# Fetching expert tokens by indirect DMA, and 512-column token-major projections, in a two-layer encoder trunk

## The chip, the cores and the metric

One core of one Trainium2 chip. The metric is device time in microseconds of one launch. The kernel before takes 1617.72 us (median of 3 runs, 1615.04 to 1621.96). The execution that was profiled took 1623.95 us.

## The reference

Two layers work on 512 tokens of 1024 features in float32. Each layer mixes tokens (gated linear attention, mLSTM and latent attention side by side, all reading the same input), projects the result back, adds a residual and normalises; then cross-attends to 256 memory tokens; then runs a mixture of experts: each token picks one of 4 groups and the two best of that group's 8 experts.

```
y = x @ w_in                                   # columns shared out among three mixers
x = LN(ALPHA * x + concat(mixers(y)) @ w_out)
x = LN(ALPHA * x + cross_attention(x, mem) @ w_o)
for e in range(32):                            # gate is 0 for all but two experts of a token
    h = silu(t @ w_gate[e]) * (t @ w_up[e])
    out = out + (h @ w_down[e]) * gate[:, e:e + 1]
x = LN(ALPHA * x + out)
```

## The kernel before, in words

Tokens are four tiles of 128. Everything but the experts is projected in three matmuls per product (`mm3`, L383): weights and activations are split into a rounded part and a rest, and hi x hi, lo x hi and hi x lo are summed in PSUM. Weights come in pieces of 128 x 1024 values (512 KB), loaded on SP's queue (L359) into `raw`, split by ScalarE (L350, `whi`) and VectorE (L351, `wlo`).

*Token-major projections.* The values and gates of two mixers (L850 to L854, L932 to L935), the output projection and the cross-attention's output projection (both in `proj_residual`, L469) give results with tokens on partitions. They are cut into groups of 256 columns: `tm_weights` (L414) splits the two pieces of a group, `tm_tile` (L417) runs 8 x 3 matmuls of 256 columns for each token tile. There are 2 + 2 + 4 + 4 groups a layer, so 12 x 4 x 24 = 1152 matmuls.

*Experts.* Every expert has 64 slots. The router (`router_tile`, L1147) gives each token's two choices a slot number. A pair of experts, 128 slots, is one iteration of the loop in `moe` (L1421), 16 a layer. A pair's weights are twelve pages of 512 KB: eight of gate and up (`in_gu`), four of down (`in_dn`). They are loaded on SP's queue (L1351) into a ring of 22 pages (`moe_raw`, L369): free pages of five tags and one tile of four pages, `raw4`, tag `T16`. A page is loaded again as soon as the matmuls that read it are done; SP issues in ring order.

TensorE's order in an iteration is the program's: the down-projection of the pair before (L1383), the up-projection of this pair (L1360), and then a last phase in which the pair before is added into the tokens (`scatter`, L1502, 16 matmuls of 512 columns, each bank then added by VectorE at L1506) and four chunks of the next four experts' tokens are gathered (`gather`, L1320). The gather is a matmul with a one-hot matrix: for each of 8 feature chunks, 2 (hi, lo) x 4 (token tiles) matmuls of 256 columns, whose one-hot VectorE builds (`slots_onehot`, L1279, `onehot_tile`, L1205). So it makes 64 matmuls for every two pairs, for slots 256 to 2047. The first 256 slots are gathered by `gather_first` (L1289) inside the router's last tiles.

*The end of a layer.* In layer 0 the last iteration starts a piece of the next layer's memory projection (`fill_ahead`, L1391), whose matmuls (tile `fb`) fill TensorE between the last scatters. Slots beyond 64 of an expert are computed after the loop in `overflow` (L1538), a loop with a count from the data: here none in layer 0, one in layer 1. GpSimd builds its one-hots (`overflow_block`, L1522 and L1523), TensorE gathers (`gather_few`, L1331) and runs one expert on 64 slots (L1558, L1571, L1580). Then comes `last_norm` (L1593).

Of the kernel before, what the change touches and what calls it, by code (L numbers as in the profile page):

```python
# [38 lines left out]
FAR = 16384  # L39
MLA_SCALE = float(96 ** -0.5)  # L40
# [69 lines left out]
def pack(x, mem, positions, w_in, w_out, gla_w_a2, gla_b_a, gla_norm_g, ml_conv_w, ml_b_i, ml_b_f, ml_norm_g,  # L110
# [23 lines left out]
    def tm(l, i, w):  # L134
        for g in range(w.shape[1] // 256):
            a = w[:, g * 256:(g + 1) * 256].reshape(2, 4, P, 256).transpose(0, 2, 1, 3).reshape(2, P, 1024)
            pieces[l, i + 2 * g:i + 2 * g + 2] = a
# [3 lines left out]
    for l in range(L):  # L141
# [18 lines left out]
        tm(l, PI_XV, arr["xkv"][l][:, D:])  # L160
# [48 lines left out]
class K:  # L209
# [50 lines left out]
    def setup(self):  # L260
        nc, a = self.nc, self.a
        self.const = self.cp.tile([P, NCO], F32, name="const")
        self.ident = self.c("ident")
        self.vec = [self.cp.tile([P, N_VC], F32, name=f"vec{l}") for l in range(L)]
        for l in range(L):
            nc.sync.dma_start(self.vec[l], a["cols"][l])
        nc.sync.dma_start(self.const, a["consts"])
        self.ones16 = self.cp.tile([P, P], F16, name="ones16")
        nc.vector.tensor_copy(self.ones16, self.c("ones"))
        self.zero16 = self.cp.tile([P, P], F16, name="zero16")  # L270
        nc.vector.memset(self.zero16, 0.0)
# [3 lines left out]
        nc.vector.tensor_copy(self.e64, self.c("e64", 1))  # L275
        self.mhalf = self.cp.tile([P, 1], F32, name="mhalf")
        nc.vector.memset(self.mhalf, -0.5)
# [91 lines left out]
    def moe_raw(self):  # L369
# [4 lines left out]
        i = self.n_raw % (len(ring) + 4)  # L374
# [4 lines left out]
        if i == len(ring):  # L379
            self.raw4 = self.t([P, 4, 1024], "T16", 4, pool=self.tp)  # L380
        return self.raw4[:, i - len(ring), :]
# [32 lines left out]
    def tm_weights(self, i, page=None):  # L414
        return [[v.rearrange("p (k c) -> p k c", k=4) for v in self.piece(i + j, page)] for j in range(2)]

    def tm_tile(self, w, xT, t):  # L417

        ps = self.bank(self.pj)[:, 0:256]
        for k in range(KC):  # L420
            self.mm3(ps, [v[:, k, t * P:(t + 1) * P] for v in xT], [v[:, k % 4, :] for v in w[k // 4]], k == 0, k == KC - 1)
# [47 lines left out]
    def proj_residual(self, l, piece0, srcT, x, ln, xT, page):  # L469
# [3 lines left out]
        st = [self.t([P, 4, 6], "ln_st", 4) for _ in range(NT)]  # L473
# [9 lines left out]
        def add(g, t, w):  # L483
            xs = x[t][:, g * 256:(g + 1) * 256]
            nc.vector.scalar_tensor_tensor(xs, xs, ALPHA, self.tm_tile(w, srcT, t), op0=OP.mult, op1=OP.add)
            nc.vector.bn_stats(st[t][:, g, :], xs)

        for g in range(2):
            w = self.tm_weights(i + 2 * g)
            for t in range(NT):  # L490
                add(g, t, w)
        w = [self.tm_weights(i + 4), self.tm_weights(i + 6, page)]
        for t in range(NT):
            for g in range(2):
                add(2 + g, t, w[g])
                if g == 0 and t:
                    finish(t - 1)
# [335 lines left out]
    def gla(self, l, xT):  # L833
# [15 lines left out]

        for t, ps in self.tm_group(base + PI_GVR, xT):  # L850
            nc.scalar.copy(V[:, t, :], ps)
        for t, ps in self.tm_group(base + PI_GVR + 2, xT):
            nc.scalar.activation(gate[:, t, :], ps, AF.Tanh, scale=0.5)
            nc.vector.scalar_tensor_tensor(gate[:, t, :], gate[:, t, :], 1.0, ps, op0=OP.add, op1=OP.mult)  # L854
# [57 lines left out]
    def mlstm(self, l, xT, mixT):  # L912
# [19 lines left out]
        for t, ps in self.tm_group(base + PI_MVO, xT):  # L932
            nc.scalar.copy(V[:, t, :, 0:64], ps.rearrange("p (h w) -> p h w", h=4))
        for t, ps in self.tm_group(base + PI_MVO + 2, xT):
            nc.scalar.activation(gate[:, t, :], ps, AF.Tanh, scale=0.5)  # L935
# [211 lines left out]
    def router_tile(self, x, t, st, r):  # L1147
# [8 lines left out]
        nc.scalar.activation(x, x, AF.Identity, scale=rs, bias=nm)  # L1156
        uT = self.t([P, KC, P], "e_y", 2, pool=self.mp)
# [121 lines left out]
    def slots_onehot(self, s, base, n):  # L1279
# [3 lines left out]
        nc.vector.tensor_scalar(sq, s, float(-base), None, op0=OP.add)  # L1283
        oh = self.t([P, NT, n], "oh", 2, F32R, self.mp)
        for t in range(NT):
            self.onehot_tile(oh[:, t, :], sq[:, t, :])
        return oh
# [24 lines left out]

    def gather(self, l, Xs, oh, n, X, chunks, run):

        nc, v = self.nc, self.vec[l]
        for f in chunks:
            ps = self.bank()[:, 0:n]
            for i in range(2):
                for t in range(NT):
                    run.append(nc.tensor.matmul(ps, X[i][t][:, f * P:(f + 1) * P], oh[:, t, :],  # L1320
                                                start=i + t == 0, stop=i + t == NT))
            self.gathered(l, Xs, f, ps)

    def gather_few(self, l, Xs, oh, X):

        nc, v = self.nc, self.vec[l]
        for hf in range(2):
            ps, rows = self.bank()[0:CAP, :], self.t([P, T], "e_s", 4, pool=self.mp)[0:CAP, :]
            for i in range(2):
                for t in range(NT):  # L1330
                    nc.tensor.matmul(ps, oh[:, t, :], X[i][t][:, hf * 512:(hf + 1) * 512], start=i + t == 0, stop=i + t == NT)  # L1331
            self.copy(rows, ps, "ad"[hf])
            ps = self.bank()
            for k in range(4):
                nc.tensor.transpose(ps[:, k * CAP:(k + 1) * CAP], rows[:, k * P:(k + 1) * P], self.ident[0:CAP, 0:CAP])
            for k in range(4):
                f = 4 * hf + k
                nc.scalar.activation(Xs[:, f, :], ps[:, k * CAP:(k + 1) * CAP], AF.Identity,
                                     scale=v[:, VC_LG + f:VC_LG + f + 1], bias=v[:, VC_LB + f:VC_LB + f + 1])
# [69 lines left out]
    def moe(self, l, r, X, x, following):  # L1409
# [3 lines left out]
        XX = self.t([P, 2, KC, 4 * CAP], "T16", 4, pool=self.tp)  # L1413
        ohs = [r["oh0"]]
        add = self.gather_first(l, XX[:, 0], ohs[0], X)
        for t in range(NT):
            add(t)
        ws = self.t([P, NE // 2], "rws")
        last = NE // 2 - 1
        self.marks, before = True, None  # L1420
        for p in range(NE // 2):  # L1421
            q, pr = p // 2, p % 2
            e = 2 * p
            if p == last:
                self.fill = iter(())
                if following and self.n_gap:
                    self.fill_ahead(following)
            up, act, turn, down, y = self.experts(
                XX[:, q % 2, :, 128 * pr:128 * pr + 128], [a["gu"][l * NE + e + i] for i in range(2)],
                [a["dn"][l * NE + e + i] for i in range(2)], ws[:, p:p + 1], self.moe_raw,  # L1430
                None if p < last else lambda: self.t([P, 1024], "e2", self.n_e2, pool=self.e2))
# [7 lines left out]
            act()  # L1439
            if p == 0:  # L1440
# [5 lines left out]
            full = []  # L1446
            if q < NE // 4 - 1:
                if pr == 0:
                    ohs.append(self.slots_onehot(s, 256 * (q + 1), 256))
                full = [lambda run, c=4 * pr + i, o=ohs[-1], X2=XX[:, (q + 1) % 2]: self.gather(l, X2, o, 256, X, (c,), run)  # L1450
                        for i in range(4)]
# [21 lines left out]
        self.overflow(l, r, X, x, sums)  # L1473
# [36 lines left out]
    def overflow_block(self, l, r, X):  # L1510
# [6 lines left out]
        o2 = self.t([P, 2, NT, 2, CAP], "oh", 2, pool=self.mp)  # L1517
        oh = self.t([P, NT, 2, CAP], "oh", 2, F32R, self.mp)
# [5 lines left out]
        self.gather_few(l, Xs, oh[:, :, 0, :], X)  # L1524
# [7 lines left out]
        for t in range(NT):  # L1532
            nc.tensor.transpose(ps[:, t * P:(t + 1) * P], oh[:, t].bitcast(F32).rearrange("p a b -> p (a b)"), self.ident)
        nc.scalar.copy(ohT, ps)
        nc.gpsimd.tensor_scalar(so, so, float(-CAP), None, op0=OP.add)
        return Xs, ws, ohT

    def overflow(self, l, r, X, x, sums):  # L1538
# [3 lines left out]
        with self.tc.For_i(0, n, 1) as i:  # L1542
# [10 lines left out]
            Xs, ws, ohT = self.overflow_block(l, r, X)  # L1553
# [144 lines left out]
    def run(self, layers=L):  # L1698
# [3 lines left out]
        self.kvd = self.dp.tile([4, P, 1024], F32, name="kvd")  # L1702
        self.early = {PI_MISC: self.raw_piece(PI_MISC)}
# [24 lines left out]
```

## Time and profile before

| | |
|---|---|
| time of the profiled execution | 1623.95 us |
| span, first to last instruction | 1622.1 us |
| granted TensorE clock, mean | 0.978 |
| busy: matmuls / weight loads | 1555.0 us (96%) / 1151.0 us (71%) |
| busy: VectorE / ScalarE / GpSimd | 1067.8 us / 575.9 us / 32.5 us |
| DMA | 303.04 MB, mean 187 GB/s |

Matmuls are pipelined, so a row's own duration is its latency; what one costs in a stream is the distance from one start to the next. TensorE is busy nearly all the time, which tells where to look but not what a change in one stage is worth: the mixers move 20 to 180 GB/s in a 40th of the span, the expert loops 240 to 380.

### The profile page before, as it was taken

The page shows a single profiled execution, that of the slowest core. Times are in us where ns is not written, and L with a number is a line of the kernel's source. Part 1 is how long each engine was busy: PE and PEld are TensorE (multiplying, and loading weights), DVE is VectorE, ACT ScalarE, POOL GpSimd, SP SyncE. Part 2 cuts the span into 40 slices and gives each one's busy share as a digit, 9 for nine tenths or more (in the row PEclk, how much of TensorE's full clock was granted, in tenths as well). Part 3 has the DMA queues.
Part 4 walks back from the last instruction along what each step waited for, and adds up shares of the span by engine and source line. Part 5 has one row for each costly group of instructions (what it writes and reads, how often), then busy time and mean ns, then how long its engine had stood idle before and what let it go on. Part 6 is the DMA issues. An engine that isn't in the chain of part 4 may idle for free. (4 is left out here: it accounts for less than half of the span.)

```text
span 1622.1 us, 25953 instructions
## 1 busy us (share of the span) xinstructions
PE 1555.0 (96%) x10270; PEld 1151.0 (71%) x10270; DVE 1067.8 (66%) x2352; ACT 575.9 (36%) x1026; POOL 32.5 (2%) x44
## 2 busy tenths in 40 slices
PE   7999999999999999999889999999999999999994
PEld 6988876898896555555579888669889855555542
DVE  6768678675568954445767857777655798545454
ACT  6434346324323222222463442552342332222212
POOL 0000000010000000000000000001000000000100
PEclk9999899999999999999999989999999999999997
DMA  6432220522437999996543332033224599899861
GB/s 218 149 119 80 79 72 20 177 68 82 155 121 268 381 341 343 342 352 247 212 152 106 104 98 93 6 122 94 92 86 153 184 351 373 326 339 346 333 238 53
DMA packets 90656, 303.04 MB, mean 187 GB/s; under 512 B 10404, under 2 KB 10916, under 8 KB 90404
## 3 DMA queue, kind: packets, MB, share of 16 engines
q1 hardware_dynamic: 90532, 301.36, 52.7%
q8 instruction: 81, 1.33, 0.3%
q14 instruction: 43, 0.35, 0.1%
HBM read 292.93 MB, written 8.39 MB: 186 GB/s over the span
## 5 line engine op out<-in xcount | busy, mean ns | idle before, releaser
L386 PE MATMUL pj<-whi,T 128*128 128x256 f32 x640 | 183.4, 287 | 4.5 <-ACT T L846 2.8
L1506 DVE TENSOR_TENSOR e<-e,sm 128x512 f32<-128x512 f32 x240 | 153.2, 683 | 51.1 <-PE sm L1502 50.7
L388 PE MATMUL pj<-wlo,T 128*128 128x256 f32 x640 | 182.9, 286 | 3.8 <-DVE wlo L351 3.8
L387 PE MATMUL pj<-whi,T 128*128 128x256 f32 x640 | 182.4, 285 | 0.0
L386 PE MATMUL pj<-T,whi 128*128 128x512 f32 (+1 forms) x368 | 135.3, 368 | 5.9 <-ACT T L350 5.6
L1502 PE MATMUL sm<-e_y,e_oT 128*128 128x512 f32 x512 | 139.3, 397 | 1.3 <-ACT e_y L1385 0.8
L351 DVE TENSOR_TENSOR wlo<-raw,whi 128x1024 fp32r<-128x1024 f32 x86 | 104.7, 1221 | 51.2 <-ACT whi L350 50.7
L387 PE MATMUL pj<-T,wlo 128*128 128x512 f32 (+1 forms) x368 | 135.9, 370 | 2.3 <-DVE wlo L351 2.3
L1320 PEld LDWEIGHTS sm<-oh,T 128*128 128x128 f32 x896 | 117.5, 188 | 25.7 <-issue 17.8
L388 PE MATMUL pj<-T,whi 128*128 128x512 f32 (+1 forms) x368 | 135.0, 368 | 0.0
L1320 PE MATMUL sm<-oh,T 128*128 128x256 f32 x896 | 129.6, 287 | 0.0
L386 PEld LDWEIGHTS pj<-whi,T 128*128 128x128 f32 x640 | 123.9, 194 | 5.8 <-ACT T L846 3.0
L388 PEld LDWEIGHTS pj<-wlo,T 128*128 128x128 f32 x640 | 123.8, 194 | 5.3 <-DVE wlo L351 5.1
L350 ACT CAST whi<-raw 128x1024 fp32r<-128x1024 f32 x86 | 89.8, 1048 | 105.2 <-PE pj L387 57.4
L387 PEld LDWEIGHTS pj<-whi,T 128*128 128x128 f32 x640 | 123.9, 194 | 0.2
L1360 PE MATMUL pj<-e,T 128*64 128x512 f32 x448 | 110.2, 593 | 0.0
L1310 ACT ACTIVATE T<-sm,vec 128x256 f32<-128x256 f32 x116 | 65.3, 566 | 105.1 <-PE sm L1320 105.1
L1502 PEld LDWEIGHTS sm<-e_y,e_oT 128*128 128x128 f32 x512 | 88.1, 188 | 20.4 <-ACT e_y L1385 3.3
L1368 DVE TENSOR_TENSOR e_sl<-e_sl,pj 128x256 f32<-128x256 f32 x32 | 13.5, 421 | 132.7 <-ACT e_sl L1367 132.6
L1385 ACT ACTIVATE e_y<-pj,rws 128x512 fp32r<-128x512 f32 x64 | 43.8, 687 | 118.6 <-PE pj L1383 106.7
L1360 PEld LDWEIGHTS pj<-e,T 128*64 128x64 f32 x448 | 35.1, 137 | 69.9 <-issue 67.7
L386 PEld LDWEIGHTS pj<-T,whi 128*128 128x128 f32 x368 | 70.5, 192 | 17.5 <-ACT T L350 6.4
(483 smaller groups left out, 3200.0 us busy)
## 6 DMA issues: line engine op xcount, KB each, us to landing
e<-in_gu SPq DMA_DIRECT2D x112, 512.0 KB, 9.3
raw<-in_pieces SPq DMA_DIRECT2D x94, 512.0 KB, 3.6
e<-in_dn SPq DMA_DIRECT2D x60, 512.0 KB, 7.6
T<-in_gu SPq DMA_DIRECT2D x44, 512.0 KB, 7.4
wlo<-in_gu SPq DMA_DIRECT2D x36, 512.0 KB, 8.9
whi<-in_gu SPq DMA_DIRECT2D x34, 512.0 KB, 8.8
raw<-in_gu SPq DMA_DIRECT2D x34, 512.0 KB, 8.5
fw<-in_pieces SPq DMA_DIRECT2D x60, 256.0 KB, 3.0
```

The source lines that it names most:

```text
L350: self.nc.scalar.copy(hi, src)
L351: self.nc.vector.tensor_tensor(lo, src, hi, op=OP.subtract)
L386: mm(ps, a[0], b[0], start=first, stop=False)
L387: mm(ps, a[1], b[0], start=False, stop=False)
L388: return mm(ps, a[0], b[1], start=False, stop=last)
L1310: self.nc.scalar.activation(Xs[:, f, :], ps, AF.Identity, scale=v[:, VC_LG + f:VC_LG + f + 1], bias=v[:, VC_LB + f:VC_LB + f + 1])
L1320: run.append(nc.tensor.matmul(ps, X[i][t][:, f * P:(f + 1) * P], oh[:, t, :], start=i + t == 0, stop=i + t == NT))
L1360: run.append(nc.tensor.matmul(st["h"][CAP * i:CAP * i + CAP, :], Xs[:, k, i * CAP:(i + 1) * CAP], st["w"][i][:, (k % 2) * 512:(k % 2 + 1) ...
L1368: nc.vector.tensor_tensor(sl[0:R], sl[0:R], st["h"][0:R, DE:], op=OP.mult)
L1385: nc.scalar.activation(y[0][0:R, c], po[0:R, :], AF.Copy, scale=ws)
L1502: m = nc.tensor.matmul(ps, ohT[:, t * P:(t + 1) * P], y[i][0:n, c], start=i == 0, stop=i == 1)
L1506: nc.vector.tensor_tensor(x[t][:, c], x[t][:, c], ps, op=OP.add)
```

## The change

In the experts, `router_tile` writes each normalised token tile to a table in DRAM (`ud`) from ScalarE's queue. For every two pairs VectorE builds the same one-hots as before, now in 16 bits; eight one-column matmuls turn them into token numbers (`slot_tokens`); and GpSimd clears a 128 x 1024 tile and fetches a pair's tokens into it by indirect DMA (`fetch`; an empty slot has a number out of bounds and stays zero). The fetch for pair p+3 is issued at the end of iteration p. In iteration p TensorE transposes the rows of pair p+1 in two groups of four (`fetched`), ScalarE applies the norm's gain and bias. `gather` and `gather_few` are gone, `gather_first` stays. As the split tokens are not read after the first gather, the ring of weight pages grows from 22 to 30. `fill_ahead` starts after the last pair's up-projection, and the last pair's down weights come from the ring. The overflow block takes its one-hots' space from `e_y`, the tag of the scatter's operands, and fetches its 64 tokens by indirect DMA.

The token-major projections take 512 columns a matmul. `tm_group` holds four banks and goes weight piece by weight piece over all four token tiles; in `proj_residual` the second half goes tile by tile, the last tile in two halves of 256.

```diff
     def moe_raw(self):
-        i = self.n_raw % (len(ring) + 4)
+        i = self.n_raw % (len(ring) + 12)
...
     def tm_group(self, i, xT):
-        w = self.tm_weights(i)
-        for t in range(NT):
-            yield t, self.tm_tile(w, xT, t)
+        ps = [self.bank(self.pj) for _ in range(3)] + [self.bank()]
+        for j in range(4):
+            w = self.tm_weights(i + j)
+            for t in range(NT):
+                for k in (2 * j, 2 * j + 1):
+                    self.mm3(ps[t], [v[:, k, t * P:(t + 1) * P] for v in xT], [v[:, k % 2, :] for v in w], k == 0, k == KC - 1)
+        return ps
...
         nc.scalar.activation(x, x, AF.Identity, scale=rs, bias=nm)
+        nc.scalar.dma_start(self.ud[self.l][t * P:(t + 1) * P, :], x)
...
+    def slot_tokens(self, s, q, oh):
+        nc.vector.tensor_scalar(sq, s, float(-256 * q), None, op0=OP.add)
         for t in range(NT):
             self.onehot_tile(oh[:, t, :], sq[:, t, :])
+        def tokens(run):
+            ps = self.bank()
+            for pr in range(2):
+                for t in range(NT):
+                    run.append(nc.tensor.matmul(ps[:, pr:pr + 1], oh[:, t, pr * P:(pr + 1) * P], self.tok16[:, t:t + 1],
+                                                start=t == 0, stop=t == NT - 1))
+            ix = self.t([P, 2], "gix", 3, I32)
+            nc.vector.tensor_scalar(ix, ps[:, 0:2], float(FARTOK), None, op0=OP.add)
+            return [ix[:, pr:pr + 1] for pr in range(2)]
+
+    def fetch(self, l, ix, n=P):
+        v = self.t([P, D], "oh", 2, pool=self.mp)[0:n]
+        self.nc.gpsimd.memset(v, 0.0)
+        self.nc.gpsimd.indirect_dma_start(v, None, self.ud[l], bass.IndirectOffsetOnAxis(ap=ix[0:n], axis=0),
+                                          bounds_check=T - 1, oob_is_err=False)
+        return v
+
+    def fetched(self, l, Xs, v, g, run):
+        n = v.shape[0]
+        ps = self.bank()
+        for k in range(4):
+            f = 4 * g + k
+            run.append(self.nc.tensor.transpose(ps[:, k * n:(k + 1) * n], v[:, f * P:(f + 1) * P], self.ident[0:n, 0:n]))
+        for k in range(4):
+            self.gathered(l, Xs, 4 * g + k, ps[:, k * n:(k + 1) * n])
...
+            tokens = None
+            if p % 2 and p + 3 <= last:
+                tokens = self.slot_tokens(s, (p + 3) // 2, oh16[:, (p + 3) // 2 % 2 ^ 1])
             ohT = self.onehot_rows(srow, p, ws)
             with self.run_of() as run:
                 for i in range(4):
+                    if i < 2 and p + 1 in rows:
+                        self.fetched(l, place(p + 1), rows[p + 1], i, run)
+                    if i == 2 and tokens:
+                        ix = tokens(run)
                     if i == 3:
                         turn(run)
-                    for f in full[i:i + 1]:
-                        f(run)
                     if before:
                         for t in (2 * i % NT, (2 * i + 1) % NT):
                             self.scatter(x, before[1], before[2], t, i // 2, run=run)
+            if 4 <= p + 3 <= last:
+                rows[p + 3] = self.fetch(l, ix[(p + 3) % 2])
...
     def overflow_block(self, l, r):
-        o2 = self.t([P, 2, NT, 2, CAP], "oh", 2, pool=self.mp)
-        oh = self.t([P, NT, 2, CAP], "oh", 2, F32R, self.mp)
+        o2 = self.t([P, 2, NT, 2, CAP], "e_y", 2, pool=self.mp)
+        oh = self.t([P, NT, 2, CAP], "e_y", 2, pool=self.mp)
...
-        self.gather_few(l, Xs, oh[:, :, 0, :], X)
+        ps = self.bank()
+        for t in range(NT):
+            nc.tensor.matmul(ps[:, 0:1], oh[:, t].rearrange("p a b -> p (a b)"), self.tok[:, t:t + 1], start=t == 0, stop=t == NT - 1)
+        ix = self.t([P, 1], "mox", dt=I32)
+        nc.vector.tensor_scalar(ix, ps[:, 0:1], float(FARTOK), None, op0=OP.add)
+        rows = self.fetch(l, ix, CAP)
```

Lines of the changed kernel stand some 11 to 23 lower: L1360 is now L1372, L1383 is L1395, L1502 is L1518.

*TensorE, last phase of an iteration.* The rows run from the end of an up-projection into the phase. Names are output, then moving operand, then weights; `T` is the split tokens, `oh` the one-hot, `e_y` and `e_oT` the scatter's operands. Before:

```order
L1360 MATMUL pj_5510<-raw_5537,T_852_5109 64x512
L1320 MATMUL sm_5604<-oh_5587,T_737_4360 128x256 x4
L1320 MATMUL sm_5604<-oh_5587,T_738_4361 128x256 x4
L1502 MATMUL sm_5614<-e_y_5494,e_oT_5409 128x512
L1502 MATMUL sm_5614<-e_y_5495,e_oT_5409 128x512
L1502 MATMUL sm_5618<-e_y_5494,e_oT_5409 128x512
L1502 MATMUL sm_5618<-e_y_5495,e_oT_5409 128x512
```

Four such blocks make the phase. Now (`oh` is the fetched rows of the next pair, the identity `const` moves):

```order
L1372 MATMUL pj_4927<-e_914_4949,T_830_4543 64x512
L1325 MATMUL sm_5005<-const,oh_4650 128x128 x4
L1518 MATMUL sm_5014<-e_y_4911,e_oT_4832 128x512
L1518 MATMUL sm_5014<-e_y_4912,e_oT_4832 128x512
L1518 MATMUL sm_5018<-e_y_4911,e_oT_4832 128x512
L1518 MATMUL sm_5018<-e_y_4912,e_oT_4832 128x512
L1325 MATMUL sm_5022<-const,oh_4650 128x128 x4
```

The eight gather matmuls of a block are gone; the first two blocks have four transposes each, the last two none. In every other pair eight one-column matmuls stand ahead of the third block.

*SP's queue at the end of layer 0's loop.* `in_gu` and `in_dn` are the last pair's weights, `in_memT` and `in_pieces` what `fill_ahead` needs, `in_rows` the last norm's gain and bias. Before:

```order
L1058 DMA whi_7416<-in_memT 128x1024
L1058 DMA wlo_7420<-in_memT 128x1024
L1351 DMA e_1387_7441<-in_gu 128x1024
L1351 DMA e_1388_7443<-in_gu 128x1024
L1351 DMA e_1389_7449<-in_gu 128x1024
```

Now:

```order
L1363 DMA raw_6702<-in_dn 128x1024
L1363 DMA raw_6704<-in_dn 128x1024
L1363 DMA raw_6706<-in_dn 128x1024
L1069 DMA whi_6712<-in_memT 128x1024
L1069 DMA wlo_6716<-in_memT 128x1024
L1612 DMA e_1354_6765<-in_rows 128x1024
L1612 DMA e_1355_6767<-in_rows 128x1024
```

The memory's loads stood ahead of the last pair's twelve pages and stand behind them now.

*GpSimd's queue in layer 1's overflow block.* Before:

```order
L1522 TENSOR_SCALAR oh_15393<-const,rs_2413_13341 128x128 x8
L1523 TENSOR_TENSOR oh_15394<-oh_15393 128x512
L1535 TENSOR_SCALAR rs_2413_13341<-rs_2413_13341 128x8
```

Now:

```order
L1538 TENSOR_SCALAR e_y_13849<-const,rs_2326_11973 128x128 x8
L1314 MEMSET oh_13867 64x1024
L1539 TENSOR_TENSOR e_y_13850<-e_y_13849 128x512
L1556 TENSOR_SCALAR rs_2326_11973<-rs_2326_11973 128x8
L1315 DMA oh_13867<-ud_78,mox_13865 64x1024
```

The one-hots moved from `oh` to `e_y`, and a memset and an indirect DMA joined the queue.

## Rows read from the trace of the kernel before

**Rows 1.** Waits of TensorE, 500 to 790 us (engine, line, what for: total, times, longest).
```profile
PE pj L1383 <- ACT e_hT L1375: 1.2, 1, 1.2
PE sm L1502 <- DVE e L1506: 0.2, 1, 0.2
```

**Rows 2.** Waits of SP's DMA queue, 500 to 800 us.
```profile
SPq L1351 <- PE pj L1383: 104.5, 16, 11.1
SPq L1351 <- PE pj L1360: 41.5, 35, 12.7
```

**Rows 3.** Timeline of TensorE: start, us, line, operation, count; one pair with gather.
```profile
577.46 1.22 PE L1320 MATMUL sm<-oh,T 128*128 128x256 f32 x8
...
595.87 1.22 PE L1320 MATMUL sm<-oh,T 128*128 128x256 f32 x8
```

**Rows 4.** The same, a pair without gather (the last but one of layer 0).
```profile
761.56 3.02 PE L1502 MATMUL sm<-e_y,e_oT 128*128 128x512 f32 x12
...
776.53 3.06 PE L1502 MATMUL sm<-e_y,e_oT 128*128 128x512 f32 x12
```

**Rows 5.** The same, eight transposes and the instruction behind them.
```profile
455.52 1.09 PE L442 MATMUL sm<-const,e 128*128 128x128 f32 x8 [0.67 <-ACT e L1156]
456.37 0.37 PE L387 MATMUL pj<-e,T 128*128 128x256 f32 x1
```

**Rows 6.** Groups by line: the gather's matmuls (count, busy, mean ns).
```profile
L1320 PE MATMUL sm<-oh,T 128*128 128x256 f32 x896 | 129.6, 287 | 0.0
```

**Rows 7.** Stretches of 20 us: busy PE, PEld, DVE, ACT, POOL; granted clock, DMA share, GB/s.
```profile
520.00:540.00 20.00, 20.00 (x108) 10.85 (x106) 19.16 (x51) 4.39 (x8) 0.00 (x0) 1.00 0.99 364
540.00:560.00 20.00, 20.00 (x110) 11.24 (x107) 19.37 (x50) 4.78 (x9) 0.00 (x0) 1.00 1.00 370
...
760.00:780.00 20.00, 19.70 (x89) 9.13 (x85) 12.94 (x21) 4.67 (x8) 0.00 (x0) 1.00 1.01 381
...
1320.00:1340.00 20.00, 20.00 (x108) 11.14 (x109) 19.52 (x51) 4.96 (x9) 0.00 (x0) 1.00 1.01 386
1340.00:1360.00 20.00, 20.00 (x108) 10.83 (x106) 19.20 (x49) 4.47 (x9) 0.00 (x0) 1.00 1.02 390
```

**Rows 8.** Timeline of TensorE: loops' first up-projections, layer 0's last down-projection, both last scatters.
```profile
497.88 7.09 PE L1360 MATMUL pj<-e,T 128*64 128x512 f32 x32
...
781.09 2.79 PE L1383 MATMUL pj<-e,e_hT 128*64 128x512 f32 x10
...
790.96 1.20 PE L1502 MATMUL sm<-e_y,e_oT 128*128 128x512 f32 x4
...
1289.04 7.09 PE L1360 MATMUL pj<-e,T 128*64 128x512 f32 x32
...
1579.49 2.11 PE L1502 MATMUL sm<-e_y,e_oT 128*128 128x512 f32 x8 [0.78 <-ACT e_y L1385]
```

**Rows 9.** Expert weight loads (L1351), whole span: issue to landing.
```profile
DMA to landing us min/median/max: 3.8/8.2/12.0
```

**Rows 10.** Timeline of GpSimd: a memset of 128 x 1024; layer 1's overflow one-hots.
```profile
811.78 0.95 POOL L865 MEMSET T<- 128x1024 f32 x1 [6.19 <-DVE T L351]
...
1504.43 5.07 POOL L1522 TENSOR_SCALAR oh<-const,rs 128x128 f32<-128x128 f32 x8 [228.86 <-PE sm L1320]
1541.29 1.29 POOL L1523 TENSOR_TENSOR oh<-oh 128x512 fp32r<-128x512 f32 x1 [31.79 <-issue]
```

**Rows 11.** Timeline of TensorE: layer 1's overflow, main run of expert matmuls.
```profile
1590.62 0.43 PE L1558 MATMUL pj<-raw,T 128*64 128x256 f32 x1
```

**Rows 12.** Timeline of TensorE: first and last of 67 matmuls of 256 columns in a stream.
```profile
60.05 0.28 PE L388 MATMUL pj<-wlo,T 128*128 128x256 f32 x1
...
67.97 0.28 PE L388 MATMUL pj<-wlo,T 128*128 128x256 f32 x1
```

**Rows 13.** The same, first and last of 8 matmuls of 512 columns.
```profile
36.65 0.39 PE L387 MATMUL pj<-T,wlo 128*128 128x512 f32 x1
...
38.24 0.39 PE L388 MATMUL pj<-T,whi 128*128 128x512 f32 x1
```

More of the change, by code (lines that the diff above doesn't have):

```diff
@@ L39 @@
 FAR = 16384
+FARTOK = 1024
 MLA_SCALE = float(96 ** -0.5)
@@ L132, in fm, with tm @@
             pieces[l, i + k] = w[:, k * P:(k + 1) * P].reshape(KC, P, P).transpose(1, 0, 2).reshape(P, -1)
[L134 to L137, printed above, removed]
+    def tm(l, i, w, n=512):
+        m = n * KC // 1024
+        for g in range(w.shape[1] // n):
+            a = w[:, g * n:(g + 1) * n].reshape(m, KC // m, P, n).transpose(0, 2, 1, 3).reshape(m, P, 1024)
+            pieces[l, i + m * g:i + m * g + m] = a
     arr = {k: np.asarray(v) for k, v in dict(
@@ L472, in proj_residual @@
         gb = None if ln is None else self.lnvec(l, ln)
-        st = [self.t([P, 4, 6], "ln_st", 4) for _ in range(NT)]
+        st = [self.t([P, 4, 6], "ln_st", 4)[:, 0:2 if t < NT - 1 else 4] for t in range(NT)]
         def finish(t):
@@ L481, in proj_residual, with add @@
         i = l * N_PIECES + piece0
[L483 to L492, printed above, removed]
+        def add(t, c, ps):
+            xs = x[t][:, c]
+            nc.vector.scalar_tensor_tensor(xs, xs, ALPHA, ps, op0=OP.mult, op1=OP.add)
+            w = 512 if t < NT - 1 else 256
+            for g in range(c.start, c.stop, w):
+                nc.vector.bn_stats(st[t][:, g // w, :], x[t][:, g:g + w])
+        for t, ps in enumerate(self.tm_group(i, srcT)):
+            add(t, slice(0, 512), ps)
+        w = [self.tm_weights(i + 4 + j, page if j > 1 else None) for j in range(4)]
         for t in range(NT):
-            for g in range(2):
-                add(2 + g, t, w[g])
-                if g == 0 and t:
+            for c in (0,) if t < NT - 1 else (0, 256):
+                cs = slice(c, c + 512 if t < NT - 1 else c + 256)
+                add(t, slice(512 + cs.start, 512 + cs.stop), self.tm_tile(w, srcT, t, cs))
+                if c == 0 and t:
                     finish(t - 1)
@@ L1311, in gathered @@
                                   bias=v[:, VC_LB + f:VC_LB + f + 1])
[L1313 to L1339, printed above, removed]
     def experts(self, Xs, gu, dn, ws, page, dpage=None):
@@ L1412, in moe @@
         s = r["s"]
-        XX = self.t([P, 2, KC, 4 * CAP], "T16", 4, pool=self.tp)
-        ohs = [r["oh0"]]
-        add = self.gather_first(l, XX[:, 0], ohs[0], X)
+        XX = self.t([P, 4, 1024], "T16", 4, pool=self.tp)
+        first = XX[:, 0:2].rearrange("p a b -> p (a b)").rearrange("p (k s) -> p k s", k=KC)
+        place = lambda n: (first[:, :, 128 * n:128 * n + 128] if n < 2 else
+                           XX[:, n % 3].rearrange("p (k s) -> p k s", k=KC))
+        oh16 = XX[:, 3].bitcast(F16).rearrange("p (i t s) -> p i t s", i=2, t=NT)
+        add = self.gather_first(l, first, r["oh0"], X)
         for t in range(NT):
             add(t)
+        ix = self.slot_tokens(s, 1, oh16[:, 0])([])
+        rows = {2 + i: self.fetch(l, ix[i]) for i in range(2)}
         ws = self.t([P, NE // 2], "rws")
@@ L1439, in moe @@
             act()
+            if p == last:
+                self.fill = iter(())
+                if following and self.n_gap:
+                    self.fill_ahead(following)
             if p == 0:
@@ L1702, in run @@
         self.kvd = self.dp.tile([4, P, 1024], F32, name="kvd")
+        self.ud = [self.dp.tile([T, D], F32, name=f"ud{l}") for l in range(layers)]
         self.early = {PI_MISC: self.raw_piece(PI_MISC)}
```

65 lines of the change are left out of this document (28 added, 37 removed).

## The prediction

> **What bounds the kernel now.** I read the page's totals first: TensorE is busy 96% of the span, so wherever its work goes away without a new wait, time goes with it. That mean says nothing of what comes next, so the second view is the waits in layer 0's expert loop, on both sides of the weight pages. TensorE waits there 1.4 us in 290, and never for a DMA [rows 1]. SP's queue waits 104.5 and 41.5 us for TensorE to give pages back [rows 2]. TensorE is the bound, and the loads have slack. How much of each there is, the third and fourth views tell. The timeline gives a pair with the gather 595.87 - 577.46 = 18.41 us [rows 3], and one without it 776.53 - 761.56 = 14.97 us [rows 4]. Twelve pages of 0.524 MB are 6.29 MB, so a pair needs 342 GB/s now. The windows of 20 us in which DMA is busiest show what it can give: 364 to 390 GB/s, at a share of 0.99 to 1.02 and a granted clock of 1.00 [rows 7]. DMA is within some 10% of its own limit, although TensorE hides it.
>
> **The gather.** Each pair loses 32 gather matmuls and gains eight transposes and, every second pair, eight one-column matmuls. Eight transposes took 456.37 - 455.52 = 0.85 us from their start to the next matmul [rows 5]. No row has one-column matmuls; between nothing and a gather matmul's stream cost, (18.41 - 14.97) / 32 = 0.11 us each, eight are 0 to 0.9 us; I take 0.5 us, 0.25 a pair. TensorE's pair is then 14.97 + 0.85 + 0.25 = 16.07 us, 2.34 less. The group of the gather has 896 matmuls [rows 6], 14 pairs in each of two layers, so TensorE alone would save 14 x 2.34 = 33 us a layer.
>
> **The transfers.** A fetch adds a thirteenth page to a pair: 6.82 MB in 16.07 us is 424 GB/s, above every window [rows 7]. So the bound changes hands, and the loop must be summed by bytes. At the loop's start the ring has 22 pages loaded, in both kernels, since the eight new pages come free with the first gather only. 170 pages, 14 fetches and two rows of norm parameters remain: 89.1 + 7.3 + 1.05 = 97.5 MB. Layer 0's full windows have 364, 370 and 381, mean 372 GB/s; layer 1's 386 and 390, mean 388 [rows 7]. So the last page lands after 262 us in layer 0 and 251 in layer 1. Then follow the last down-projection and scatter, 792.16 - 781.09 = 11 us (790.96 + 1.20 is their end). Layer 0's loop takes 273 us instead of 792.16 - 497.88 = 294.3; layer 1's takes 262 instead of 1581.60 - 1289.04 = 292.6 [rows 8]. That is **-21 and -30 us**. All 33 us come only if DMA moves 97.5 MB in 294.3 - 33 - 11 = 250 us, 390 GB/s throughout, the best window there is. The larger ring moves nothing of this sum: it lets SP run further ahead, but a queue that is always full has no use for that.
>
> **What waits newly.** *The fetch.* Its chain is a memset, 0.95 us [rows 10], the index from TensorE and VectorE, and a transfer; expert pages took 3.8 to 12.0 us to land [rows 9]. An indirect DMA has no row; between 4 and 12 us, I take the upper end, since it lands among full queues: some 14 us with the index. It may take nearly two pairs, some 32 us, as two buffers alternate and the transposes come two phases later. So it costs nothing; if it takes longer, the transposes hold TensorE's whole queue. The memset of the next fetch stands behind it on GpSimd, which has nothing else there. *The loop's start.* The first fetches wait for one-hots and the token matmuls, 0 to 2.5 us on TensorE a layer; I take 1, nearer to nothing because they stand behind the first up-projection of 7.09 us [rows 8]: **+2**. *Layer 0's end.* The memory's loads stand behind the last pages instead of ahead of them, and two rows behind those. What filled TensorE between the last scatters comes later, by nothing if the loads land before the last scatter, by 6 us if they don't (four pages' landing at 372 GB/s): **+3**. *Layer 1's overflow.* The one-hots, 5.07 + 1.29 us on GpSimd [rows 10], were made long before they were needed, in a space that nothing held. In `e_y` they wait for the last scatter, which ends at 1581.60 [rows 8], and memset, token matmuls, index, fetch and transposes follow them. The experts' matmuls begin now at 1590.62, 9 us after that scatter [rows 11]. The new chain is 5.07 + 0.95 + 1.29 plus a landing of 3.8 at the least and about 1.5 for matmuls, index and transposes, 12.6 us; with a landing of 12.0 it is 21. So +3.6 to +12; the queues are empty there, so I take **+6**, nearer the low end.
>
> Costed at nothing: ScalarE applies the norm in 16 pieces of 128 columns instead of 8 of 256, half the columns each, and is busy 5 us in 20 [rows 7]; the next down-projection covers it, and without that cover about 2 us a pair would show. VectorE builds the same number of one-hots, one every second pair. The table's writes, 4 x 0.524 MB a layer, are 5.6 us of DMA at 372 GB/s; they fall ahead of the loop, where the page's slices show DMA far from full; in full queues they would cost these 5.6.
>
> **The 512 columns.** A stream of 256-column matmuls takes (67.97 - 60.05) / 66 = 0.1200 us each [rows 12], one of 512 columns (38.24 - 36.65) / 7 = 0.2271 [rows 13]. Of the 1152 matmuls a layer, 192 stay at 256 columns (a last tile's halves) and the others become half as many. In two layers that is 2112 taken away and 1056 put in: 1056 x (0.2400 - 0.2271) = **-13.6 us**. If the groups' ends, where VectorE now gets its tiles close together, give it back, it is 0; if stalls between groups go too, some 18.
>
> **The sum.** -21 - 30 + 2 + 3 + 6 - 13.6 = -54 us on the profiled execution, whose span of 1622.1 us lies in a time of 1623.95. That is 0.4% above the median; I take the difference over unchanged: 1617.7 - 54 = **1564 us**. With layer 0 at 364 or 381 GB/s and the costs at their ends, 1550 to 1580.
>
> **The rivals.**
>
> *DMA gives more.* If a queue that is never starved by SP's waits sustains 390 GB/s or more, TensorE stays the bound: -66 + 11 - 14 = -69, 1549 us; with the small costs at 3 and the columns at 18, 1537. For it: SP's 146 us of waits [rows 2] mean the queue ran dry at times. Against it: in the windows I used the share is already 1.0, and layer 0's stay at 364 to 381 [rows 7]. Chance 0.20.
>
> *DMA gives less.* If the lowest full window, 364 GB/s, holds in both layers, the bytes take 268 us, the loops save 15 and 14, and the sum is -29 + 11 - 14 = -32: 1586 us. For it: rows of 4 KB for scattered tokens need not move as well as pages. Against it: layer 1's windows at 386 and 390 [rows 7]. Chance 0.14. The Trainium skill's page DMA: Bandwidth & Descriptors, section Specifications, puts a core's share of the memory at about 358 GB/s; by that the loops would save 11 and 9 us, and the time would be 1595. The windows of rows 7 are all above that figure, so the trace speaks against the rule as a ceiling here.
>
> *No gain.* If 342 GB/s, what a pair moves today, is all that DMA gives with a second queue issuing into the same engines, the bytes take 285 us and the loops 296: +2 and +3; with +11 and -14 that is 1620. The same comes out where the fetches' bytes displace pages one for one. Windows above 364 at a full share [rows 7] speak against it. Chance 0.06.
>
> *The fetch becomes the bound, and it is slower.* With two buffers a pair can't be shorter than half a fetch, memset to landing. The point from which that decides against the change is 2 x 18.41 = 37 us: at 40 us a fetch, a pair takes 20, 14 x 1.59 = 22 us more a layer than now, and the time is 1617.7 + 44 + 11 - 14 = 1659. For it: no row shows GpSimd issue a DMA, and VectorE is busy up to 19.5 us in 20 beside it [rows 7]. Against it: the nearest rows sum to 14 us. Chance 0.08. The Trainium skill's page SBUF — State Buffer, section SBUF: two separate sides, says that descriptors of a DMA issued on GpSimd are written by its cores, which some VectorE operations lock out of a shared port; no row here shows it.
>
> **How the numbers follow.** The forecast keeps 0.52. A measurement of this kernel tells about 0.5%, 8 us, from no change. Forecast and the first two rivals are all faster by more: 0.86; no gain is 0.06, slower 0.08. The range must hold 8 in 10: the forecast, most of the case of more bandwidth down to 1538, and that of less bandwidth up to 1597; left out are no gain, the slow fetch and a little of the lower end.
>
> **What would show it.** Right: windows in the loops at 370 GB/s or more at a share of 1.0; TensorE waiting at its projections for `in_gu` or `in_dn` DMAs, where it never did; SP's waits for TensorE much smaller; eight transposes 0.85 us apart from the next matmul; fetches landing within 15 us and no wait at the transposes; 512-column matmuls 0.227 us apart in the projections; the overflow's one-hots behind the last scatter and its matmuls 12 to 16 us after it. Wrong: TensorE without DMA waits (then DMA gives more, and pairs take 16.1 us); waits at the transposes for the fetch; pairs of 18 us at 364 GB/s or less; or projections whose groups end in waits for VectorE that eat the 13.6 us.

## The result and the profile after

The changed kernel takes 1558.45 us (median of 4 runs, 1552.75 to 1561.04) against 1616.38 before: a ratio of 0.9633, interval 0.9593 to 0.9674, 58 us less where 54 were forecast. The range held. The mechanism did not: TensorE is still the bound of the expert loops, as the first rival had it, and the number came out near by errors that cancel.

First the totals and the slices of the page after (the last two rows are the granted clock in tenths and GB/s).

```profile
PE 1478.3 (95%) x8646; PEld 1011.7 (65%) x8646; DVE 1054.6 (68%) x2316; ACT 592.0 (38%) x1137; POOL 88.3 (6%) x102
...
PEclk9999899999999999999899999999999999999996
...
GB/s 227 143 129 82 89 75 21 167 63 108 138 126 273 414 412 413 413 411 279 171 128 109 110 102 75 28 66 158 82 95 174 203 332 413 413 413 413 411 136 55
```

TensorE's busy share has hardly moved; each loop is five slices at 411 to 414 GB/s. Windows of 20 us, as in [rows 7]:

```profile
520.00:540.00 20.00, 19.77 (x93) 8.29 (x90) 18.37 (x46) 6.32 (x14) 1.95 (x2) 1.00 1.03 412
540.00:560.00 20.00, 19.72 (x100) 8.53 (x98) 18.79 (x49) 5.11 (x13) 1.94 (x2) 1.00 1.03 414
...
1320.00:1340.00 20.00, 19.77 (x96) 8.80 (x93) 16.83 (x46) 5.95 (x15) 1.95 (x2) 1.00 1.03 413
```

Is DMA now what TensorE waits for? The waits of TensorE in layer 0's loop, 500 to 744 us, answer to [rows 1]:

```profile
PE sm L1518 <- ACT T L1350: 1.4, 3, 1.0
PE pj L1395 <- ACT e_hT L1387: 0.7, 1, 0.7
PE sm L1518 <- DVE e_y L1398: 0.4, 1, 0.4
PE sm L1518 <- DVE e L1522: 0.4, 2, 0.2
```

No DMA among them. SP's queue has turned round: in [rows 2] it waited 146 us for TensorE to free pages; in layer 0's loop now (500 to 744) the largest totals are for transfers that it issued before. The one long wait for TensorE, 15.7 us, stands at the loop's end, ahead of the norm's rows.

```profile
SPq L1363 <- DMA T<-in_gu: 45.3, 46, 2.0
SPq L1363 <- DMA e<-in_gu: 33.4, 34, 2.7
...
SPq L1363 <- PE sm L1518: 5.5, 19, 0.4
SPq L1363 <- PE pj L1395: 2.1, 7, 0.4
```

The timeline of TensorE gives the pair, from one down-projection to the next, and inside it the eight transposes and the eight one-column matmuls:

```profile
568.54 3.65 PE L1395 MATMUL pj<-T,e_hT 128*64 128x512 f32 x16
...
579.00 0.66 PE L1325 MATMUL sm<-const,oh 128*128 128x128 f32 x4
579.41 1.17 PE L1518 MATMUL sm<-e_y,e_oT 128*128 128x512 f32 x4
580.42 0.60 PE L1325 MATMUL sm<-const,oh 128*128 128x128 f32 x4
580.90 1.19 PE L1518 MATMUL sm<-e_y,e_oT 128*128 128x512 f32 x4
581.93 0.35 PE L1304 MATMUL sm<-tok,T 128*128 128x1 f16 x8
582.41 1.19 PE L1518 MATMUL sm<-e_y,e_oT 128*128 128x512 f32 x4
...
584.68 0.64 PE L1395 MATMUL pj<-e,e_hT 128*64 128x512 f32 x1
...
600.62 3.65 PE L1395 MATMUL pj<-T,e_hT 128*64 128x512 f32 x16
```

Pairs of 16.14 us with the token matmuls and 15.94 without, mean 16.04 where the forecast had 16.07. Transposes: 0.41 + 0.48 = 0.89 (0.85 forecast); token matmuls 0.48 (0.5).

The span in stages, cut at each loop's first up-projection and last scatter as in [rows 8], in us, with two of the experiments below:

| stage | before | changed | columns alone | fetch alone |
|---|---|---|---|---|
| to layer 0's loop | 497.9 | 486.9 | 483.6 | 497.9 |
| loop, layer 0 | 294.3 | 268.5 | 293.9 | 267.4 |
| to layer 1's loop | 496.9 | 492.1 | 488.2 | 501.6 |
| loop, layer 1 | 292.5 | 265.8 | 292.9 | 265.4 |
| to the end | 40.5 | 46.0 | 40.5 | 45.6 |

Where an experiment leaves the loops as they are, they repeat within 2 us. The stages between them don't: the changed kernel in another run had 483.0 and 486.5 us for the first and third. Stretches at 1.2 GHz come and go there: from 165 to 175 us the granted clock was 0.50 in the one profile, 0.97 or more in the other. So what a change does to those stages is judged by the medians of the whole time.

### The profile page after: what moved, and what is told of

Same layout as the page of the kernel before. It is cut to its first block, busy times and chain, and to the rows that moved or that the text cites. A ratio compares the mean times of both kernels' runs of the same rounds, so it can differ in the third digit from the quotient of the medians.

```text
span 1559.2 us, 22997 instructions
## 1 busy us (share of the span) xinstructions
PE 1478.3 (95%) x8646; PEld 1011.7 (65%) x8646; DVE 1054.6 (68%) x2316; ACT 592.0 (38%) x1137; POOL 88.3 (6%) x102
## 5 line engine op out<-in xcount | busy, mean ns | idle before, releaser
L1518 PE MATMUL sm<-e_y,e_oT 128*128 128x512 f32 x512 | 153.4, 422 | 7.7 <-ACT T L1350 2.9
L1518 PEld LDWEIGHTS sm<-e_y,e_oT 128*128 128x128 f32 x512 | 85.0, 189 | 43.8 <-ACT e_hT L1387 8.6
L393 PE MATMUL pj<-whi,T 128*128 128x512 f32 (+1 forms) x272 | 105.1, 386 | 5.5 <-ACT T L859 5.2
L395 PE MATMUL pj<-wlo,T 128*128 128x512 f32 (+1 forms) x272 | 104.1, 385 | 0.8 <-DVE wlo L357 0.8
L394 PE MATMUL pj<-whi,T 128*128 128x512 f32 (+1 forms) x272 | 104.0, 382 | 0.0
L1372 PE MATMUL pj<-e,T 128*64 128x512 f32 x376 | 92.3, 596 | 0.0
L1380 DVE TENSOR_TENSOR e_sl<-e_sl,pj 128x256 f32<-128x256 f32 x32 | 13.5, 421 | 115.5 <-ACT e_sl L1379 115.4
L1350 ACT ACTIVATE T<-sm,vec 128x128 f32<-128x128 f32 (+2 forms) x236 | 85.9, 467 | 5.1 <-PE sm L1325 5.1
L1372 PE MATMUL pj<-T,T 128*64 128x512 f32 x384 | 85.5, 592 | 0.0
L393 PEld LDWEIGHTS pj<-T,whi 128*128 128x128 f32 x368 | 71.8, 195 | 18.9 <-ACT T L356 6.9
L394 PEld LDWEIGHTS pj<-T,wlo 128*128 128x128 f32 x368 | 71.7, 195 | 13.6 <-DVE wlo L357 2.8
L395 PEld LDWEIGHTS pj<-T,whi 128*128 128x128 f32 x368 | 71.6, 195 | 11.4 <-issue 0.9
L1398 DVE SCALAR_TENSOR_TENSOR e_y<-pj,rws,e_y 128x512 fp32r<-128x512 f32 x64 | 47.8, 749 | 36.1 <-ACT e_y L1397 36.0
L356 ACT CAST fwh<-fw 128x512 fp32r<-128x512 f32 x60 | 37.2, 620 | 90.3 <-PE fb L394 36.2
```

The costliest lines, as they stand in the source:

```text
L356: self.nc.scalar.copy(hi, src)
L393: mm(ps, a[0], b[0], start=first, stop=False)
L394: mm(ps, a[1], b[0], start=False, stop=False)
L395: return mm(ps, a[0], b[1], start=False, stop=last)
L1350: self.nc.scalar.activation(Xs[:, f, :], ps, AF.Identity, scale=v[:, VC_LG + f:VC_LG + f + 1], bias=v[:, VC_LB + f:VC_LB + f + 1])
L1372: run.append(nc.tensor.matmul(st["h"][CAP * i:CAP * i + CAP, :], Xs[:, k, i * CAP:(i + 1) * CAP], st["w"][i][:, (k % 2) * 512:(k % 2 + 1) ...
```

## The experiments

**The two parts apart.** `cols_only` is the kernel before with the new layout of the weights, `tm_weights`, `tm_tile`, `tm_group` and `proj_residual`; `fetch_only` is everything else of the diff.

> The kernel before with the 512-column projections alone. If a 512-column matmul simply costs 0.2271 us where two of 256 cost 0.2400 (the forecast's term), the time falls by 13.6 us to about 1603. If the groups' ends or the clock give part of it back, as the two traces' stretches outside the expert loops suggest (some 11 us less in all), it falls by 8 to 12. If they give all of it back, no change. The expert loops keep pairs of 18.4 us.

Measured: 1595.71 against 1615.08, ratio 0.9882 (0.9861 to 0.9903), -19.4 us: more than either expectation. The column "columns alone" shows that the loops are untouched. The streams are as forecast: in `cols_only` long streams of 512-column matmuls have 0.227 to 0.231 us from one start to the next. What the sum had left out are waits. Those ahead of TensorE's transposes, over the whole span, were before (the part of the line's view that says what it sat idle for):

```profile
  ACT e L1156: 2.5, 7
  DVE e L458: 2.5, 6
```

and are in `cols_only`:

```profile
  DVE e L463: 0.8, 2
```

In `proj_residual` a token tile's norm and transposes stand behind the first group of the next tile: 24 matmuls of 256 columns, 2.9 us, which did not cover the norm's chain (an addition, statistics, two passes). 24 of 512 columns, 5.5 us, do. That is 4.2 us; two other waits in the view rise by 0.3 each, so it explains 3.6 of the 5.8 that the streams leave. The rest is within the interval.

> The kernel before with the fetch (and its larger ring and later fill) alone. If the two parts don't touch each other, it gains what the whole change does less the columns: -44 to -50 us, 1566 to 1572. Theory T (TensorE stays the bound of the loops, DMA gives 410 GB/s and more): pairs of 16.1 us, no TensorE wait for a DMA in the loops, windows of 20 us at 405 to 415 GB/s. Theory D (the forecast: DMA becomes the bound at 372 and 388 GB/s): TensorE waits there for in_gu and in_dn.

Measured: 1576.02, ratio 0.9749 (0.9726 to 0.9772), -39.1 us; 5 less than expected. The two parts add up: -19.4 - 39.1 = -58.5, and the whole change gave 58. The loops show theory T: 267.4 and 265.4 us, and no TensorE wait for a DMA.

That the time comes near the forecast's -21 - 30 + 11 = -40 is chance. The two loops alone are 54 us shorter and the stage to the end is 5 longer, -49 together, so some 10 us came back in the other two stages. The granted clock of whole runs goes with them: 0.968 to 0.979 in the five of `fetch_only`, 0.982 to 0.985 in the eleven of the kernel before beside them, 0.981 to 0.985 in the six of `cols_only`. No experiment followed them to a place, so their cause stays open.

**What DMA can give.** `ring22` takes the larger ring away; `extra1` and `extra2` load one or two more pages a pair, which nothing reads.

```diff
-        i = self.n_raw % (len(ring) + 12)
+        i = self.n_raw % (len(ring) + 4)
...
+                for _ in range(2):
+                    load(dn[0][:, 0:1024], page)
                 st["w"] = [[load(d[:, k * 1024:(k + 1) * 1024], dpage or page) for d in dn] for k in range(2)]
```

> The changed kernel with the ring of weight pages kept at 22. Theory T with a queue that needs depth (the eight more pages are what keeps DMA at 413 GB/s): SP waits for TensorE again, 20 us windows fall to 370 to 400 GB/s, TensorE waits for weights, each layer's loop is 5 to 15 us longer, 1569 to 1588 in all. Theory T without depth (413 GB/s is what DMA gives whenever pages are asked for, and the fetch's second queue or the shorter pairs ask for them): within 5 us of 1558, SP's waits for TensorE come back without effect. The forecast said that the larger ring moves nothing.

Measured: 1555.73, ratio 0.9619 (0.9584 to 0.9655): the changed kernel's time. Windows from 520 us on stay at 405 to 417 GB/s, and TensorE has no wait for a DMA. SP's waits for TensorE come back in part (500 to 744 us; 2.1 us in this line with the ring of 30), but none of these is longer than 3.8 us, where [rows 2] has 11.1:

```profile
SPq L1363 <- PE pj L1395: 12.0, 17, 3.8
```

The ring moves nothing, as forecast.

> The changed kernel with one more 0.524 MB weight page loaded in each pair, which nothing reads: 8.4 MB a layer. Theory T (ceiling 413 GB/s): the last page of layer 0 lands some 17 us before its down-projection now, and 8.4 MB take 20.3 us, so each loop is about 3 us longer: +4 to +10 us, 1562 to 1568. If DMA were already the bound of the loops (the forecast), every byte counts: +20 us a layer, 1599.

Measured: 1566.39, ratio 0.9690 (0.9656 to 0.9724), 8 us above the changed kernel: theory T. The 16 pages a layer are 20 us of DMA, and the loops grew by 4.3 and 2.8.

> The changed kernel with two such pages in each pair, 16.8 MB a layer. Theory T with a ceiling of 413 GB/s: 40.6 us of DMA less 17 of slack, +23 us a layer, 1605 in all, and TensorE waits for in_gu and in_dn in the loops. If the ceiling is higher (430 GB/s), +12 a layer, 1582; if DMA was the bound already, +41 a layer, 1640.

Measured: 1599.18, ratio 0.9890 (0.9854 to 0.9925): 41 us above the changed kernel, the loops at 285.5 and 286.1 us, +17 and +20. Here DMA is the bound at last, and a window shows what it gives then:

```profile
670.00:690.00 20.00, 19.45 (x89) 9.17 (x88) 9.49 (x17) 6.28 (x16) 2.74 (x3) 1.00 1.03 413
```

413 GB/s again, with TensorE short of weights: that is the ceiling in these runs. The forecast's formula holds here with this rate: (97.5 + 16.8) / 0.413 + 11 = 288 us, for 286 measured. The changed kernel's queue runs at the ceiling too, but ahead of TensorE: of the 40.6 us of added transfers 17.0 and 20.3 show, which leaves 20 to 24 us of slack in each loop; `extra1` by the same subtraction has 16 to 18, the 17 expected. How a reader sees the shortage is worth a look, since TensorE is "busy" 19.45 us of 20 in that window. A matmul's record is its latency, which covers most gaps between two; the last six pairs of the loop take 18.1 us on average, and the waits stand with the weight loads (500 to 762 us of `extra2`):

```profile
PEld pj L1372 <- DMA T<-in_gu: 9.8, 16, 1.1
...
PEld pj L1372 <- DMA e<-in_gu: 4.9, 12, 1.1
...
PEld pj L1372 <- DMA raw<-in_gu: 3.8, 5, 1.1
```

In the changed kernel the weight loads' largest row for a DMA (500 to 744 us) has no wait over 0.4 us, and the steady pairs of 15.94 and 16.14 us leave no room for more.

```profile
PEld pj L1395 <- DMA T<-in_gu: 1.9, 6, 0.4
```

**The fetch's slack.** `slow_fetch` puts ten more memsets ahead of each fetch of a pair.

```diff
-        self.nc.gpsimd.memset(v, 0.0)
+        for _ in range(11 if n == P else 1):
+            self.nc.gpsimd.memset(v, 0.0)
```

> The changed kernel with ten more memsets on GpSimd ahead of each fetch of a pair, 9.5 us of it. In the trace a fetch's DMA starts 30 us ahead of the transposes that read it and lands in 7: theory T says that there are some 20 us of slack, so nothing changes (within 3 us of 1558). The rival of the slow fetch: if the fetch is within 9 us of setting the pair, TensorE waits at the transposes and each pair grows, by up to 9.5 / 2 us, 14 x 4.7 x 2 = 130 us in all.

Measured: 1564.61, ratio 0.9679 (0.9644 to 0.9714), some 6 us above the changed kernel (the intervals overlap), outside the 3 expected and nowhere near 130. The steady pairs are the same, 15.95 and 16.15 us, and TensorE doesn't wait at the transposes: the slack is there. What shows stands at the loops' start: the loops are 3.4 and 2.2 us longer, and in layer 0 TensorE waits 2.7 us there for the first pair's activations from VectorE, some of whose operations take longer in that run (the last section).

**The end of layer 1 and the start of the loops.** `early_onehots` takes two free weight pages for the overflow's one-hots; `early_rows` writes the 32 matmuls that make rows of the slots and gates ahead of the first up-projection; `rows_onehots` does both.

```diff
-        o2 = self.t([P, 2, NT, 2, CAP], "e_y", 2, pool=self.mp)
-        oh = self.t([P, NT, 2, CAP], "e_y", 2, pool=self.mp)
+        o2, oh = (self.t([P, 1024], "e2", self.n_e2, pool=self.e2) for _ in range(2))
...
         add = self.gather_first(l, first, r["oh0"], X)
+        srow = self.token_rows(s) + self.token_rows(self.gates(r))
...
-                srow = self.token_rows(s) + self.token_rows(self.gates(r))
```

> The changed kernel with the overflow block's one-hots in two weight pages that are free by then instead of e_y. If their wait for the last scatter is what the tail of layer 1 lost (5.5 us more from the last scatter to the end than before), GpSimd makes them before the loop ends and the tail gets 5 to 6 us shorter: 1552 to 1553. Rival: the fetch's own chain (index, GpSimd's DMA, landing) is the longer one and takes the place of the wait: 0 to 2 us gained.

Measured: 1558.95, ratio 0.9653 (0.9631 to 0.9674). The stage to the end fell from 46.0 to 41.0 us as expected, but the time did not move. In the profiled execution the first and third stages were 3.1 us longer together than the changed kernel's, at granted clocks of 0.97 and 0.96 against 0.98 and 0.97, and the runs of either kernel spread over 5 us and more. This is inconclusive by itself; `rows_onehots` below has the same edit again, beside a repeat of the changed kernel.

> The changed kernel itself, on the chip that the two runs beside it use, so that a few microseconds can be told. 1553 to 1562.

Measured: 1554.02, ratio 0.9631 (0.9609 to 0.9654).

> The changed kernel with the 32 matmuls that turn slot numbers and gates into rows written ahead of the first up-projection, so that they stand among the router's last steps on TensorE, as in the kernel before, and not behind that projection. Theory: they filled 3 to 4 us in which TensorE now waits for VectorE, and that idleness brings the clock down to 1.2 GHz in the first up-projection (9.2 us there against 7.0). Then from the last router tile to the first down-projection layer 0 gets some 4 us shorter and layer 1 some 2: 1549 to 1555. Rival: the waits for VectorE are on the path whatever stands between them, and the rows come out of the same time elsewhere: within 2 us of the changed kernel.

Measured: 1549.87, ratio 0.9584 (0.9559 to 0.9608), 4 us less. Here is what it removes, in the repeated changed kernel: the router's last steps and the first up-projection.

```profile
477.88 0.25 PE L1251 MATMUL sm<-rM,ones 128*128 128x32 f16 x4 [1.16 <-DVE rV L1212]
479.24 2.90 PE L1340 MATMUL pj<-oh,T 128*128 128x256 f32 x12 [1.12 <-DVE oh L1220]
481.94 1.05 PE L1340 MATMUL sm<-oh,T 128*128 128x256 f32 x4
482.80 0.26 PE L1304 MATMUL sm<-tok,T 128*128 128x1 f16 x2
482.98 1.97 PE L1372 MATMUL pj<-e,T 128*64 128x512 f32 x2
484.88 0.31 PE L1304 MATMUL sm<-tok,T 128*128 128x1 f16 x6
485.12 7.08 PE L1372 MATMUL pj<-e,T 128*64 128x512 f32 x30
492.13 2.05 PE L1284 MATMUL sm<-const,rs 128*128 128x128 f32 x16
```

TensorE waits 1.16 and 1.12 us for VectorE, and then twelve matmuls of 256 columns take 2.70 us from their start to the next row, where [rows 12] has them at 0.12 each: the granted clock was 0.51 from 480 to 485 us. With the rows early, the same place reads:

```profile
473.89 0.25 PE L1251 MATMUL sm<-rM,ones 128*128 128x32 f16 x4 [0.26 <-DVE rV L1212]
474.12 0.72 PE L1284 MATMUL sm<-const,rs 128*128 128x128 f32 x4
475.29 2.05 PE L1284 MATMUL sm<-const,rw 128*128 128x128 f32 x16 [0.44 <-ACT e_s L1287]
477.09 1.64 PE L1340 MATMUL pj<-oh,T 128*128 128x256 f32 x12
```

The waits are filled and the twelve run at full speed. From the router's last row (L1179) to the first down-projection it is 20.9 us against 23.9. Not all of the theory holds: the idleness moves on, 2.37 us ahead of the first transposes in the loop, and the slow clock with it (0.50 from 490 to 495 us).

> The same with the overflow block's one-hots in free weight pages as well. If the 5 us by which that shortened the stretch after layer 1's last scatter are worth as much in the time, 5 us below the run with early rows, some 1547. If the clock gives them back in the last 40 us, the same time as that run.

Measured: 1545.09, ratio 0.9559 (0.9539 to 0.9579): another 4.8 us, so the shorter stage to the end (40.6 us, 46.5 with the early rows alone) is worth nearly as much in the time as in the profile. It is the fastest version, 9 us below the changed kernel beside it; their intervals don't touch. Its GpSimd starts on the one-hots 19 us before the last scatter ends, at 1502.40, and TensorE then waits for the fetch alone:

```profile
1483.27 4.68 POOL L1539 TENSOR_SCALAR e<-const,rs 128x128 f32<-128x128 f32 x8 [38.53 <-PE pj L1372]
...
1505.13 1.02 POOL L1315 DMA_INDIRECT oh<-ud,mox  x1 [14.81 <-DVE mox L1545]
```

```profile
1509.84 1.09 PE L1325 MATMUL sm<-const,oh 64*128 64x64 f32 x8 [3.93 <-DMA oh<-ud,mox]
```

## Why the prediction was right, and where not

*What bounds the loops: wrong.* The step that failed is "the windows of 20 us in which DMA is busiest show what it can give: 364 to 390 GB/s". They show a mean over stretches at full rate and dips. SP waited in those same windows: each of the five in [rows 7] has one wait of 4.4 to 6.1 us for a down-projection. From 520 to 540 us, before,

```profile
SPq L1351 <- PE pj L1383: 6.1, 1, 6.1
```

and the DMA view of before, 520 to 700 us in 40 slices, has the dips and the ceiling side by side:

```profile
GB/s 321 389 414 328 381 409 413 330 321 419 411 263 346 412 412 228 363 419 408 162 386 416 410 162 369 338 404 256 345 416 416 214 260 339 420 350 344 378 413 256
```

It reaches 405 to 420 again and again, and falls to 162 between. Around that first wait SP issued nothing from 525.5 to 533.0 us; the rate stood at 401 to 426 GB/s from 526 to 534, fell to 176 and 295 in the next two us, and was back at 401. The share of 0.99 to 1.02 that counted as proof of a full queue is not one: the windows at 413 have 1.03, and these few hundredths went with 6 to 12% of the rate. In the dip itself the share hardly moves (the last three numbers are granted clock, share, GB/s):

```profile
534.00:535.00 1.00, 1.00 (x8) 0.33 (x6) 1.00 (x3) 0.60 (x1) 0.00 (x0) 1.00 1.02 176
```

The rate of 413 was there to be read before the change. By the forecast's own formula it is 97.5 / 0.413 + 11 = 247 us, less than the 261 that TensorE needs. The first rival was right, and its reason (SP's waits) too; the prediction had also named its sign, pairs of 16.1 us without a DMA wait. The Trainium skill, page DMA: Bandwidth & Descriptors, section Specifications, has about 358 GB/s for a core's share; the windows at 413 in the changed kernel and in `extra2` speak against that as a ceiling here.

*The loops' saving: near in sum, by two errors against each other.* Forecast 273 and 262 us, measured 268.5 and 265.8. With TensorE as the bound the forecast's terms give 33 us a layer, and 25.8 and 26.7 came. The pair was right (16.04 for 16.07), their number wasn't. Of the 14 gathers, one stood in the first iteration; its 3.4 us did not come off, since the rows and the waits of the loop's start took the place: from the first up-projection to the first down-projection it was 511.79 - 497.88 = 13.9 us before,

```profile
511.79 0.64 PE L1383 MATMUL pj<-e,e_hT 128*64 128x512 f32 x1 [1.25 <-ACT e_hT L1375]
```

and is 500.85 - 486.90 = 13.9 now. And the first pair after that took 519.35 - 500.85 = 18.5 us, not 16; its scatters wait 0.45 us for VectorE and 0.97 for ScalarE. The loop's start was costed at +1 a layer; by these two it is some 3.4 + 2.4 = 6. `early_rows` shows a part of it undone: with the rows gone from it, the first iteration takes 489.93 - 479.32 = 10.6 us up to the first down-projection.

*The fetch: right.* Landings of 2.8, 7.1 and 8.7 us (least, median, longest) for the 4 to 12 taken, a memset of 0.95, no wait at the transposes, and `slow_fetch` shows the slack. The rival of the slow fetch is out.

*Layer 0's end: smaller.* +3 forecast; from the last down-projection to the last scatter's end it is 755.38 - 743.69 = 11.7 us instead of 11.1.

*Layer 1's overflow: right.* +6 forecast, +5.5 in the stage. The experts' matmuls begin 13.5 us after the last scatter, against 9.0 [rows 8, 11], and `early_onehots` shows that the wait is the one named, for the one-hots behind the last scatter:

```profile
1519.33 1.87 PE L1542 MATMUL sm<-tok,e_y 128*128 128x1 f32 x8 [6.11 <-POOL e_y L1539]
...
1526.68 1.98 PE L1581 MATMUL pj<-raw,T 128*64 128x256 f32 x8
```

*The 512 columns: mis-sized.* -13.6 forecast, from the streams; -19.4 measured alone and -17.6 on top of the fetch (1576.02 to 1558.45). The streams' 0.0129 us a matmul held; the waits for the norm went too. The bound of 18 had allowed for it. (The 192 matmuls that stay at 256 columns are those of both layers, not of one; 2112 and 1056 follow from that.)

*The sum: near by luck.* The loops came out 52.6 us shorter, where the forecast has -21 - 30 + 2 + 3 = -46; the columns gave 18 to 19, the last stage cost 5.5. That is -65 to -66, and the time fell by 58. So 7 to 9 us came back in the stages between the loops, for which the forecast had no term; `fetch_only` shows 10 there by the same count. The granted clock of whole runs was 0.970 to 0.980 with the changed kernel (nine runs) and 0.979 to 0.985 before (29 runs beside the experiments). A part of the difference is the last stage's, already counted (0.65 now, 0.75 before, in the profiles); no experiment followed the rest to its place, and the cause of these 7 to 9 us stays open.

## What to carry to other kernels

Read a transfer ceiling from the finest slices in which the queue was not held back, with the issuer's waits beside them; a window that holds a long wait can show what the kernel asked for, not what DMA can give. When work leaves a loop, count how many iterations really lose it: the first and the last have waits of their own, into which the saving can vanish. And a longer run of matmuls between a result and its consumer pays twice, in the stream and in the waits that it covers.

## What the runs showed of the hardware

*GpSimd's memsets slow some of VectorE's operations.* In `slow_fetch` VectorE's comparisons of a tensor with a scalar took twice as long on average, and operations with two tensors in SBUF did not change. Groups by line, 500 to 745 us, changed kernel:

```profile
L1220 DVE SCALAR_TENSOR_TENSOR T<-const,gsq,T 128x256 f16<-128x256 f32 x16 | 7.5, 479 | 0.1
...
L1219 DVE TENSOR_SCALAR T<-const,gsq 128x256 f16<-128x256 f32 x16 | 5.3, 349 | 0.0
```

`slow_fetch`:

```profile
L1219 DVE TENSOR_SCALAR T<-const,gsq 128x256 f16<-128x256 f32 x16 | 11.0, 710 | 0.0
L1220 DVE SCALAR_TENSOR_TENSOR T<-const,gsq,T 128x256 f16<-128x256 f32 x16 | 7.6, 483 | 0.1
```

Single ones took 1.0 us there, about a memset (0.95). The Trainium skill, page SBUF — State Buffer, section SBUF: two separate sides, says that a GpSimd instruction and some of VectorE's take a shared port pair for the whole instruction, and that VectorE's with two inputs in SBUF do so only against a GpSimd instruction that reads SBUF. These rows agree with it, since a memset only writes. No run isolated the cause further.

*Short waits came with a slower clock behind them.* In the repeated changed kernel 2.3 us of waiting for VectorE came with granted clocks of 0.81 and 0.51 in the two stretches of 5 us from 475; with other matmuls in the waits' place the clock stayed at full there, and was 0.50 behind the next wait, of 2.37 us.
